# The down product of both feed-forward blocks in seven products, one product after the other over all tokens

## The chip, the cores and the metric

The kernel runs on one NeuronCore of a Trainium2 chip. The metric is the device time of one execution in microseconds (us), from the first instruction to the last output in DRAM. The core has five instruction streams that matter here: PE (matrix products into PSUM banks), DVE and POOL (elementwise work), ACT (elementwise work with functions and row sums) and SP, which only issues DMA transfers. Each stream runs its instructions in order and waits at semaphores for the others. [...]

## The reference

One encoder layer is applied to 1280 tokens (256 of a prompt, 1024 of a sample) of width 1024. What matters here is the feed-forward block, which stands at both ends of the layer:

```python
def swiglu(x, w_gu, w_down):
    g, u = jnp.split(x @ w_gu, 2, axis=-1)
    return (jax.nn.silu(g) * u) @ w_down

x = x + 0.5 * rmsnorm(swiglu(rmsnorm(x, ffn1_pre), ffn1_w_gu, ffn1_w_down), ffn1_post)
...   # attention in two head groups, with projections in and out
x = x + 0.5 * rmsnorm(swiglu(rmsnorm(x, ffn2_pre), ffn2_w_gu, ffn2_w_down), ffn2_post)
x = rmsnorm(x, final_norm)
```

`w_gu` is 1024 x 5632 and `w_down` 2816 x 1024. All inputs and outputs are float32.

## The kernel before

**Numbers.** Every large product takes its float32 operands as a rounded part and a rest (`split`: ACT copies the rounded part, DVE subtracts it from the source), and does three matmuls for one: high x high, high x low, low x high.

**Gate and up phase** (class `GateUp`). The tokens are ten tiles of 128, taken in five pairs; chunk 0 holds two pairs and chunk 1 three, so that a matmul has 256 or 384 columns, one token of each pair in either half. The hidden width is 22 blocks f of 128. For each block and chunk the gate and up product of the two halves of the model width and the two tokens of a pair is done in Strassen's form (Winograd's variant), in seven products j = 0..6 of 12 matmuls: a block is 2 x 7 x 12 = 168 matmuls (L289). The sums of the weight halves are made on DVE during the block before (L258 to L267), and each of seven weight operands is split (L63 on ACT, L66 on DVE). Each product is added from its PSUM bank into an SBUF tile by DVE (L298) or copied by ACT. At j = 5 and 6 the hidden values `w` (the first token of each pair) and `v` (the second) are ready (L312, L317) and stored to DRAM, two DMAs to a chunk, in planes `hd`. SP also issues the next gate and up weights, `raw`, 2 x 512 KB to a block, at the end of a block.

**Down phase** (class `Down`, `down_phase`). The 22 blocks are in four groups `FGROUPS`. The output width is in two halves. For half 0 and then half 1, token tile by token tile, `part` multiplies the four groups of hidden values (`hl` loaded from `hd`, split into `hh` and `hl`) with the weights `wd`, which stay in SBUF for all ten tiles, into one PSUM bank: 2 halves x 10 tiles x 22 blocks x 3 = 1320 matmuls of 512 columns to a phase (L390). Weights arrive as `rawd`, 256 KB each, through two buffers, 44 to a phase. `first_done` takes the sum of squares of half 0 (ACT) and puts it into DRAM (`y0d`). `second_done` and `finish` are a chain by token tile: squares of half 1 (ACT, L163), the row factor (POOL, L171 and L172), the two halves scaled (DVE, L1150, L1151), added to the residual (L1153, L1154), squares of the sum (ACT), a second row factor (POOL) and the scaling with it (DVE: L1258 in the first phase, L1352 in the second). In the first phase the tile is then transposed on PE and split (L76, L77, L81) as operand `xt` of the attention's projection (`pj`, L519), whose weights `mraw` come by SP (L502); in the second phase it is the output.

**Order.** The code is one stream of calls with generators (`yield`) that interleave; a scheduler of the framework then sets the order in each engine's stream, and inserts the waits. A tile of a pool with n buffers waits until the n-th before it has been released. So the order on DVE and SP around a place is read from the built program, as below.

## Time and profile before

| What | us |
|---|---|
| median of 3 runs (lowest, highest) | 2406.21 (2404.09, 2406.82) |
| the profiled execution | 2410.93 |
| its span, first to last instruction | 2409.2 |
| PE busy | 2321.3 |
| DVE busy | 1336.0 |
| ACT busy | 940.9 |
| POOL busy | 393.0 |
| first down phase, first to last matmul | 599 to 917 |
| second down phase, first to last matmul | 2089 to 2397 |

In the lines below, a group of instructions is named by its line in the kernel before, its engine and operation, and output <- inputs by the program's names; then come its count, its busy time, the mean of one in ns, and the idle time ahead of it with what ended it. A timeline row has the start and length in us. A row of windows has the stretch, its length, PE's busy time with the number of matmuls that started in it, the granted clock, the share of time the DMA engines were busy, and GB/s.

### The profile page before, as it was taken

Reading aid. Unit: us, or ns where it says so; the run is one execution under the profiler, and the core shown is the slowest. Engines: PE = TensorE matmul, PEld = TensorE weight load, DVE = VectorE, ACT = ScalarE, POOL = GpSimd, SP = SyncE. Lnnn points to the kernel's source line nnn. Section 1 sums busy time; section 2 is a strip of 40 time slices with the busy share of each in tenths; the row PEclk is TensorE's granted clock in tenths of the full one; section 3 lists DMA queues with packets and bytes.
Section 4 is the critical chain, followed back from the end, with each engine's and each line's share of the span. In section 5 each row is a group of like instructions: output and inputs, shape, how many; then the busy total and the mean of one; then the engine's idle time right before and its main releaser. Section 6 shows DMA issues by size and latency. Waiting matters only on the chain.

```text
span 2409.2 us, 36473 instructions
## 1 busy us (share of the span) xinstructions
PE 2321.3 (96%) x13658; PEld 2119.2 (88%) x13658; DVE 1336.0 (55%) x2459; ACT 940.9 (39%) x1937; POOL 393.0 (16%) x548
## 2 busy tenths in 40 slices
PE   6999999999999998999999898899999999999997
PEld 5999999999778886888888787799999999978885
DVE  7665545555443552697655764755555555552344
ACT  5322222223442332587655754422222233342232
POOL 6000000000000112585433424500000000000011
PEclk9999999999999999999999999999999999999999
DMA  4254344533654552322432454322222223463544
GB/s 137 68 122 106 90 120 114 118 76 103 194 176 156 166 182 87 84 56 64 127 101 74 162 172 155 132 81 62 80 64 77 65 69 91 138 219 113 188 163 135
DMA packets 308514, 282.40 MB, mean 117 GB/s; under 512 B 64816, under 2 KB 248496, under 8 KB 308336
## 3 DMA queue, kind: packets, MB, share of 16 engines
q1 hardware_dynamic: 308336, 280.06, 39.8%
q8 instruction: 108, 1.77, 0.3%
q14 instruction: 70, 0.57, 0.1%
HBM read 207.51 MB, written 75.24 MB: 117 GB/s over the span
## 4 chain that ended last, share of the span: by engine, by line
PE 46%; DMA 5%; DVE 4%; POOL 2%; ACT 2%; issue 2%; SPq 0%; DVEq 0%; POOLq 0%; ACTq 0%
PE gups L289 21%; PE pj L519 9%; PE dps L390 6%; PE yps L984 3%; DMA hl<-hd 2%; PE s_ps L548 2%; PE pt L558 2%; DMA rawd<-in_ffn_w_down_dram 1%; ACT junk L163 1%; PE ssq L969 1%; PE o_ps L675 1%; DMA out_dram<-xr 1%; DVE stk L66 1%; POOL rs L172 1%; DVE sb L531 0%
## 5 line engine op out<-in xcount | busy, mean ns | idle before, releaser
L289 PE MATMUL gups<-xh,ah 128*128 128x256 f32 (+1 forms) x2464 | 763.2, 310 | 7.6 <-ACT ah L63 3.3
L289 PE MATMUL gups<-xh,al 128*128 128x256 f32 (+1 forms) x2464 | 761.7, 309 | 0.0
L289 PE MATMUL gups<-xl,ah 128*128 128x256 f32 (+1 forms) x2464 | 761.2, 309 | 0.0
L390 PE MATMUL dps<-wd,hh 128*128 128x512 f32 x1760 | 547.0, 392 | 5.8 <-ACT wd L63 2.8
L289 PEld LDWEIGHTS gups<-xh,ah 128*128 128x128 f32 x2464 | 468.6, 190 | 10.8 <-ACT ah L63 4.1
L289 PEld LDWEIGHTS gups<-xh,al 128*128 128x128 f32 x2464 | 468.4, 190 | 0.6 <-DVE al L66 0.2
L289 PEld LDWEIGHTS gups<-xl,ah 128*128 128x128 f32 x2464 | 468.7, 190 | 0.0
L390 PEld LDWEIGHTS dps<-wd,hh 128*128 128x128 f32 x1760 | 329.5, 188 | 80.2 <-ACT hh L63 6.6
L390 PE MATMUL dps<-wd,hl 128*128 128x512 f32 x880 | 344.8, 392 | 2.6 <-DVE hl L66 2.3
L66 DVE TENSOR_TENSOR hl<-hl,hh 128x768 fp32r<-128x768 f32 (+1 forms) x160 | 142.2, 891 | 243.0 <-ACT hh L63 211.6
L171 POOL TENSOR_SCALAR rs<-ssq,ss 128x1 f32<-128x1 f32 x20 | 9.5, 475 | 1422.7 <-ACT junk L163 1422.7
L63 ACT ACTIVATE hh<-hl 128x768 fp32r<-128x768 f32 (+1 forms) x160 | 126.7, 793 | 279.7 <-DMA hl<-hd 252.7
L390 PEld LDWEIGHTS dps<-wd,hl 128*128 128x128 f32 x880 | 165.6, 188 | 43.5 <-DVE hl L66 9.6
L63 ACT ACTIVATE ah<-s 128x512 fp32r<-128x512 f32 x176 | 111.0, 631 | 218.9 <-PE gups L289 140.7
L66 DVE TENSOR_TENSOR al<-s,ah 128x512 fp32r<-128x512 f32 x176 | 121.6, 691 | 95.0 <-ACT ah L63 93.8
L519 PE MATMUL pj<-xh,mh 128*128 128x512 f32 (+1 forms) x432 | 162.1, 375 | 1.8 <-ACT mh L63 1.8
L519 PE MATMUL pj<-xh,ml 128*128 128x512 f32 (+1 forms) x432 | 155.6, 360 | 0.0
L519 PE MATMUL pj<-xl,mh 128*128 128x512 f32 (+1 forms) x432 | 155.2, 359 | 0.0
L542 POOL TENSOR_TENSOR sb<-sb,rc 128x384 f32<-128x384 f32 (+1 forms) x160 | 126.3, 810 | 153.5 <-DVE rc L540 140.6
L316 ACT ACTIVATE u<-u 128x256 f32<-128x256 f32 x88 | 41.4, 471 | 254.8 <-DVE u L298 250.8
L63 ACT ACTIVATE ah<-raw 128x512 fp32r<-128x512 f32 x132 | 83.2, 630 | 134.6 <-PE gups L289 126.9
L298 DVE TENSOR_TENSOR u<-u,gups 128x384 f32<-128x384 f32 (+1 forms) x176 | 85.5, 486 | 71.7 <-PE gups L289 70.0
(154 smaller groups left out, 3152.3 us busy)
## 6 DMA issues: line engine op xcount, KB each, us to landing
raw<-in_ffn_w_gu_dram SPq DMA_DIRECT2D x88, 512.0 KB, 4.0
hl<-hd SPq DMA_DIRECT2D x80, 384.0 KB, 3.7
hl<-hd SPq DMA_DIRECT2D x80, 320.0 KB, 3.3
rawd<-in_ffn_w_down_dram SPq DMA_DIRECT2D x88, 256.0 KB, 3.1
tab<-tt SPq DMA_DIRECT2D x24, 384.0 KB, 3.5
hd<-w SPq DMA_DIRECT2D x44, 192.0 KB, 2.2
hd<-v SPq DMA_DIRECT2D x44, 192.0 KB, 2.1
tt<-zd SPq DMA_DIRECT2D x16, 384.0 KB, 6.0
```

Of the source, the lines that this page charges most:

```text
L63: nc.scalar.activation(hi, src, AF.Copy)
L66: (lo_eng or nc.vector).tensor_tensor(lo, src, hi.bitcast(F32), op=ALU.subtract)
L163: c.nc.scalar.activation(junk[:, :x.shape[1]], x, AF.Square, scale=1 / 32, accum_out=ss)
L289: nc.tensor.matmul(ps, w[:, k, :], x[:, k, :], start=new and k == 0 and m == 0, stop=k == 3 and m == 2, skip_group_check=not new)
L298: nc.vector.tensor_tensor(out, x, ps, op=add)
L316: nc.scalar.activation(X["u"], X["u"], AF.Silu)
L390: nc.tensor.matmul(ps, a[:, i, :], b, start=f == 0 and m == 0, stop=f == NFF - 1 and m == 2)
L519: nc.tensor.matmul(ps[:, :n], w[:, kk, :], xs[th][:, kk, :], start=first, stop=last)
L542: nc.gpsimd.tensor_tensor(s, s, rc[:, i:i + 1].to_broadcast(list(s.shape)), op=ALU.mult)
L548: nc.tensor.matmul(o, q, kk, start=z == 0, stop=z == 1)
L558: nc.tensor.transpose(pt[:, b, :], sbs[i][:, b * 128:(b + 1) * 128], c.ident)
L984: nc.tensor.matmul(ps, a[:, j, i * 128:i * 128 + 128], b, start=j == 0 and m == 0, stop=j == 3 and m == 2)
```

## The change

The down product too is done in seven products. With the hidden width in two halves (blocks 0 to 10 and 11 to 21), the output width in two halves, and the two tokens of a pair as the two rows, it is a product of 2 x 2 blocks, and `DOWN7` lists the operands of the seven products: hidden planes `w0`, `v0`, `w1`, `v1` (token of the pair, half) or sums `s1` to `s4` of them, and weight blocks B11, B21, B22 or sums T1 to T4 of them. All sums are made on POOL during the gate and up phase: `sums` for each block f >= 11 and chunk (the planes of block f - 11 are fetched back from DRAM, four additions, four stores), and `weight_sums` for the down weights in each odd block (three loads, four additions of 512 columns, four stores).

The down phase goes product by product (q), within it pair by pair (p), within it in two pieces (m) of 6 and 5 blocks. One product of a pair is 11 x 3 = 33 matmuls into one bank, and DVE adds it into accumulators in SBUF (`plus`; four tiles to a pair). The first 44 weight loads of a phase become 77. The second token of each pair is complete at q = 4, the first at q = 6, and the chain (`tile_done`, `finish`) runs behind these two. In the first phase the transposes of the q = 4 tiles are issued together at part 60, and those of the very last tile inside `mix_attention`, whose first loop takes its third stretch of eight steps before its second. PSUM in this phase is four banks for the products and four for the transposes.

```diff
-FGROUPS = [range(0, 6), range(6, 12), range(12, 17), range(17, 22)]
+HF = NFF // 2
+PIECES = [range(0, 6), range(6, 11)]
+PLANES = ("w0", "v0", "w1", "v1", "s1", "s2", "s3", "s4")
+DOWN7 = [("w0", "B11"), ("s2", "T2"), ("s3", "T3"), ("v1", "T4"), ("s1", "T1"), ("s4", "B22"), ("w1", "B21")]
 ...
@@ GateUp
+            self.store("v", f, ch, X["v"])
+            if f >= HF:
+                self.sums(f, ch)
 ...
+    def fetch(self, f, ch):
+        n = CN[ch]
+        x = self.G.tile([128, 2, 384], F32, name="back", tag="x", bufs=3)
+        self.back = [x[:, i, :n] for i in range(2)]
+        for i, name in enumerate(("w0", "v0")):
+            self.c.nc.sync.dma_start(self.back[i].rearrange("p (r x) -> p r x", x=128), self.plane(name, f, ch))
+
+    def sums(self, f, ch):
+        n, e, sub, add = CN[ch], self.c.nc.gpsimd.tensor_tensor, ALU.subtract, ALU.add
+        x = self.G.tile([128, 2, 384], F32, name="sums", tag=("ga", "gb")[ch], bufs=1)
+        s3, s4 = [x[:, i, :n] for i in range(2)]
+        w0, v0 = self.back
+        w1, v1 = self.X["w"], self.X["v"]
+        e(s3, w0, v0, op=sub)
+        self.store("s3", f, ch, s3)
+        e(v0, v0, v1, op=add)
+        self.store("s1", f, ch, v0)
+        e(w0, v0, w0, op=sub)
+        self.store("s2", f, ch, w0)
+        e(s4, w1, w0, op=sub)
+        self.store("s4", f, ch, s4)
 ...
@@ Down
+    def weight_sums(self, i):
+        nc, w = self.c.nc, self.w_down
+        e, sub = nc.gpsimd.tensor_tensor, ALU.subtract
+        x = self.G.tile([128, 2, 512], F32, name="bx", tag="x", bufs=3)
+        nc.sync.dma_start(x.rearrange("p s d -> p (s d)"), w[i * 128:(i + 1) * 128])
 ...
+        e(b22, b22, b12, op=sub)
+        nc.sync.dma_start(self.td["T3"][i], b22)
+        e(b12, b12, b11, op=sub)
+        nc.sync.dma_start(self.td["T1"][i], b12)
+        e(b11, b22, b11, op=ALU.add)
+        nc.sync.dma_start(self.td["T2"][i], b11)
+        e(b21, b21, b11, op=sub)
+        nc.sync.dma_start(self.td["T4"][i], b21)
 ...
     def part(self, n):
+            for v, (a, b) in enumerate(((hi, wh), (hi, wl), (lo, wh))):
+                nc.tensor.matmul(ps, a[:, k, :], b, start=i == 0 and v == 0, stop=i == HF - 1 and v == 2)
+        if m == 0:
+            return
+        A = self.acc[p]
+        def plus(out, x):
+            if out not in A:
+                A[out] = self.ap.tile([128, 512], F32, name=f"{out}{p}")
+            if x is None:
+                nc.scalar.activation(A[out], ps, AF.Copy)
+            else:
+                nc.vector.tensor_tensor(A[out], A[x], ps, op=ALU.add)
 ...
+        if q == 0:
+            plus("c11", None)
+        elif q == 1:
+            plus("u", "c11")
+        elif q == 2:
+            plus("v", "u")
+        elif q == 3:
+            plus("c21", "v")
+            sq("c21", 0)
+        elif q == 4:
+            plus("v", "v")
+            sq("v", 1)
+            plus("u", "u")
+        elif q == 5:
+            plus("u", "u")
+            sq("u", 2)
+        else:
+            plus("c11", "c11")
+            sq("c11", 3)
 ...
@@ mix_attention
-        for i in range(0, 24, 8):
+        for i in (0, 16, 8):
+            if i == 8:
+                late()
 ...
@@ encoder
+    def block_hooks(gu, f, extra):
 ...
+        def behind():
+            with tc.issue_after(gu.last_load.ins):
+                d.weight_sums(f // 2)
+        if f % 2:
+            hooks[10] = behind
+        if f == NFF - 1:
+            for n, i in ((0, 0), (1, 1), (2, 2), (3, 3), (7, 4), (8, 5), (9, 6), (11, 7), (12, 8), (13, 9)):
+                old = hooks.get(n)
+                hooks[n] = lambda old=old, i=i: (old and old(), d.load_w(0, i))
 ...
@@ down_phase
+        for n in range(len(d.seq)):
+            q, p, m = d.seq[n]
 ...
+            if n == 60:
+                last()
+            if m == 0 and q in (4, 6):
+                t = PAIRS[p][q == 4]
+                x = G.tile([128, D], F32, name="xr", tag="x", bufs=3)
+                nc.sync.dma_start(x, res(t))
+            d.load_h(n + 1)
+            d.load_h(n + 2)
+            d.part(n)
+            while loads and done < (2.2 * (n + 1) if n < 10 else 22 + 1.1 * (n - 9)):
+                loads.pop(0)()
+                done += 1
 ...
@@ finish1
-        xn = G.tile([128, D], F32, name="xn", tag="x", bufs=3)
-        nc.vector.scalar_tensor_tensor(xn, x, r, gain, op0=ALU.mult, op1=ALU.mult)
+        for y, h in halves:
+            nc.vector.scalar_tensor_tensor(y, x[:, h], r, gain[:, h], op0=ALU.mult, op1=ALU.mult)
 ...
+        elif t == PAIRS[-1][0]:
+            th, off = third(t)
+            x = state["xt"][1][th][:, :, off:off + 128].bitcast(F32)
+            for k, y in enumerate(xn):
+                nc.sync.dma_start(x[:, 4 * k:4 * k + 4], y.rearrange("p (k x) -> p k x", x=128))
+            state["xn"][t] = [x[:, 4 * k:4 * k + 4] for k in range(2)]
+            state["late"] = transposes(t)
```

The first place is DVE in the second down phase, at the token tiles near its end. Names: `dps` is a product's bank, `xr` the residual, `y`, `c` and `u` result halves, `rs` a row factor. Before, one tile:

```order
L1150 SCALAR_TENSOR_TENSOR y_22820<-y_22820,rs,ga 128x512 [waits DMAHW0_49,Pool_49]
L1151 SCALAR_TENSOR_TENSOR y_22927<-dps,rs,ga 128x512 [waits Activation_49]
L1153 TENSOR_TENSOR xr<-xr,y_22820 128x512 [waits DMAHW3_49,DMAHW5_49,DMAHW2_49,DVE_49]
L1154 TENSOR_TENSOR xr<-xr,y_22927 128x512 [waits DVE_49]
L66 TENSOR_TENSOR hl<-hl,hh 128x640 [waits DMAHW7_49,PE_49,Activation_49]
L1352 SCALAR_TENSOR_TENSOR xr<-xr,rs,gb 128x512 [waits Activation_49,Pool_49]
L1352 SCALAR_TENSOR_TENSOR xr<-xr,rs,gb 128x512 [waits DVE_49]
```

Now, one pair at q = 6:

```order
L477 TENSOR_TENSOR c_22334<-c_22334,dps 128x512 [waits PE_49]
L71 TENSOR_TENSOR hl<-hl,hh 128x640 [waits DMAHW5_49,Activation_49]
L1263 SCALAR_TENSOR_TENSOR c_22334<-c_22334,rs,ga 128x512 [waits Activation_49,Pool_49]
L1263 SCALAR_TENSOR_TENSOR u_22661<-u_22661,rs,ga 128x512
L1266 TENSOR_TENSOR xr<-xr,c_22334 128x512 [waits DVE_49]
L1266 TENSOR_TENSOR xr<-xr,u_22661 128x512 [waits DVE_49]
L71 TENSOR_TENSOR hl<-hl,hh 128x768 [waits DMAHW0_49,Activation_49]
L1467 SCALAR_TENSOR_TENSOR xr<-xr,rs,gb 128x512 [waits Activation_49,Pool_49]
L1467 SCALAR_TENSOR_TENSOR xr<-xr,rs,gb 128x512 [waits DVE_49]
L477 TENSOR_TENSOR c_22400<-c_22400,dps 128x512 [waits PE_49]
```

The addition of the next pair's product stands behind the last scaling of this pair's chain, with two waits for POOL between; half as many matmuls lie between two tiles as before.

The second place is SP at the end of the first down phase. Before:

```order
L1254 DMA x1d_75<-xr 128x1024 [waits DMAHW0_49,DVE_49]
L575 DMA cos<-in_cosT_dram 128x1024 [waits PE_49]
L577 DMA sin<-in_sinT_dram 128x1024 [waits DMAHW2_49,PE_49]
L579 DMA mA<-in_maskA_dram 128x384 [waits DMAHW3_49]
L1254 DMA x1d_76<-xr 128x1024 [waits DMAHW4_49,DVE_49]
L581 DMA sk<-in_sink_a_dram 128x8 [waits DMAHW5_49]
L502 DMA mraw<-in_w_in_dram 128x8x128 [waits DMAHW6_49,PE_49]
L502 DMA mraw<-in_w_in_dram 128x8x128 [waits DMAHW7_49]
```

Now:

```order
L1369 DMA x1d_69<-xr 128x1024 [waits DVE_49]
L1369 DMA x1d_71<-xr 128x1024 [waits DMAHW5_49,DMAHW4_49,DVE_49]
L1369 DMA x1d_73<-xr 128x1024 [waits DMAHW1_49,DVE_49]
L1382 DMA xl_8581<-c_7053 128x4x128 [waits DMAHW6_49,DVE_49]
L1382 DMA xl_8581<-u_7351 128x4x128 [waits DVE_49]
L678 DMA cos<-in_cosT_dram 128x1024 [waits DMAHW0_49]
L680 DMA sin<-in_sinT_dram 128x1024
L682 DMA mA<-in_maskA_dram 128x384 [waits DMAHW2_49]
L684 DMA sk<-in_sink_a_dram 128x8 [waits DMAHW3_49]
L605 DMA mraw<-in_w_in_dram 128x8x128 [waits DMAHW4_49]
L605 DMA mraw<-in_w_in_dram 128x8x128 [waits DMAHW5_49]
```

The loads of `cos`, `sin`, `mA` and `mraw` stand behind two transfers of the last tile (`xl`), which wait for DVE's last scaling; before, only `sk` and `mraw` stood behind the last tile's `x1d`.

The third place is SP in a block of the second gate and up phase. Before:

```order
L322 DMA hd_135<-w 128x3x128 [waits DVE_49]
L322 DMA hd_136<-v 128x3x128 [waits DVE_49]
L322 DMA hd_133<-w 128x2x128 [waits DMAHW6_49,DVE_49]
L322 DMA hd_134<-v 128x2x128 [waits DMAHW7_49,DVE_49]
L238 DMA raw<-in_ffn_w_gu_dram 128x8x128 [waits DMAHW0_49,DMAHW2_49,DVE_49,Activation_49]
L238 DMA raw<-in_ffn_w_gu_dram 128x8x128 [waits DMAHW3_49,DMAHW1_49,DVE_49]
```

Now, a block with f >= 11:

```order
L336 DMA hd1s_153<-sums 128x2x128 [waits DMAHW2_49,Pool_49]
L243 DMA raw<-in_ffn_w_gu_dram 128x8x128 [waits DMAHW3_49,DVE_49,Activation_49]
L243 DMA raw<-in_ffn_w_gu_dram 128x8x128 [waits DMAHW4_49,DVE_49]
L403 DMA bt<-in_ffn_w_down_dram 128x512
L404 DMA bt<-in_ffn_w_down_dram 128x512
L336 DMA hd1w_138<-w 128x3x128 [waits DMAHW7_49,DVE_49]
L336 DMA hd1v_142<-v 128x3x128 [waits DMAHW0_49,DVE_49]
L336 DMA hd1s_146<-back 128x3x128 [waits DMAHW1_49,Pool_49]
L336 DMA hd1s_150<-back 128x3x128 [waits DMAHW2_49,Pool_49]
L336 DMA hd1s_158<-sums 128x3x128 [waits DMAHW3_49,Pool_49]
L399 DMA bx<-in_ffn_w_down_dram 128x1024 [waits DMAHW4_49,DMAHW2_49,DMAHW1_49]
L336 DMA hd1s_154<-sums 128x3x128 [waits DMAHW5_49,Pool_49]
```

SP carries the sums' stores (`hd1s`), which wait for POOL, and the next loads of `raw` stand behind one of them.

More of the change, by code (lines that the diff above doesn't have):

```diff
@@ L334, in run @@
                 next(nxt, None)
-            if n == 6 and late:
-                late()
+            if n in hooks:
+                hooks[n]()
         for _ in nxt:
@@ L368, in load_h, with tile @@
+        def tile(name):
+            if n == 0:
+                return self.G.tile([128, 6, 128], F32R, name=name, tag="x", bufs=3)[:, :k]
+            return self.hp.tile([128, 6, 128], F32R, name=name, bufs=3)[:, :k]
+        lo, hi = tile("hl"), tile("hh")
+        nc.sync.dma_start(lo.bitcast(F32), self.hd[DOWN7[q][0]][m][ch][p - CHUNKS[ch][0]])
         split(c, hi, lo, lo.bitcast(F32))
         self.sub[n] = hi, lo
-    def order(self, entries):
-        for half, ts in entries:
-            for g in range(4):
-                self.seq += [(half, t, g) for t in ts]
-        self.n, self.ps = 0, {}
@@ L378, in part @@
-    def part(self, n, fs=None):
+    def part(self, n):
         c, nc = self.c, self.c.nc
-        half, t, g = self.seq[n]
+        q, p, m = self.seq[n]
         self.load_h(n)
         hi, lo = self.sub.pop(n)
-        if g == 0:
-            self.ps[t] = c.ps.tile([128, 512], F32, name="dps", tag="y")
-        ps = self.ps[t]
-        for i, f in enumerate(FGROUPS[g]):
-            wh, wl = self.w[half, f][:, 0], self.w[half, f][:, 1]
-            for m, (a, b) in enumerate(((hi, wh), (hi, wl), (lo, wh))):
-                nc.tensor.matmul(ps, a[:, i, :], b, start=f == 0 and m == 0, stop=f == NFF - 1 and m == 2)
@@ L1166, in encoder @@
     c.ps.use(**dict(GATE, tr=(4, 5, 6, 7)))
-    def wd_first(d):
-        for f in range(5):
-            d.load_w(0, f, G, ("x", "x", "x", "ga", "gb")[f], 3 if f < 3 else 1)
     gain = []
@@ L1234, in encoder, with open_xt @@
     for f in range(1, NFF):
-        if f == NFF - 1:
-            with tc.issue_after(gu.last_load.ins):
-                wd_first(gu.down)
-        gu.run(f, behind if late and f > 1 else None)
+        gu.run(f, block_hooks(gu, f, {6: behind} if late and f > 1 else {}))
     L.close(2)
-    R.close(2)
-    d = gu.down
-    d.hp = L.open("h", 1)
-    p0 = L.open("wd0", 1)
-    p1 = R.open("wd1", 1)
-    state = {}
-    def swap():
+    R.close()
+    state = dict(xn={}, late=None)
+    def open_xt():
         L.close(2)
@@ L1250, in swap, with transposes, finish1 @@
         state["xt"] = new_xt(c)
-        d.hp = R.open("h2", 1)
-    def finish1(t, x, gain):
+        for t in state["xn"]:
+            for _ in transposes(t):
+                pass
+    def transposes(t):
+        th, off = third(t)
+        for k, y in enumerate(state["xn"][t]):
+            pt = c.ps.tile([128, 4, 128], F32, name="tr", tag="tr")
+            for j in range(4):
+                src = y[:, j * 128:(j + 1) * 128] if len(y.shape) == 2 else y[:, j]
+                nc.tensor.transpose(pt[:, j, :], src, c.ident)
+            hi, lo = [x[th][:, 4 * k:4 * k + 4, off:off + 128] for x in state["xt"]]
+            nc.scalar.activation(hi, pt, AF.Copy)
+            nc.vector.tensor_tensor(lo, pt, hi.bitcast(F32), op=ALU.subtract)
+            yield 1
+    def finish1(t, x, gain, halves):
         nc.sync.dma_start(x1d[t], x)
```

214 lines of the change are left out of this document (107 added, 107 removed).

## The prediction

> **What bounds the kernel now.** I read the busy table, then windows by stage, then the groups of the down product.
>
> ```profile
> PE 2321.3 (96%) x13658; PEld 2119.2 (88%) x13658; DVE 1336.0 (55%) x2459; ACT 940.9 (39%) x1937; POOL 393.0 (16%) x548
> ```
> ```profile
> 100.00:500.00 400.00, 400.00 (x2723) 398.98 (x2722) 223.24 (x404) 108.25 (x211) 9.14 (x9) 1.00 0.46 108
> 1600.00:2000.00 400.00, 400.00 (x2737) 400.00 (x2737) 223.27 (x405) 110.54 (x209) 0.00 (x0) 1.00 0.24 69
> ```
> ```profile
> L390 PE MATMUL dps<-wd,hh 128*128 128x512 f32 x1760 | 547.0, 392 | 5.8 <-ACT wd L63 2.8
> L390 PE MATMUL dps<-wd,hl 128*128 128x512 f32 x880 | 344.8, 392 | 2.6 <-DVE hl L66 2.3
> ```
>
> PE is busy 96% of the span. The second fence holds windows of all engines (PE, PE's weight loads, DVE, ACT, POOL, then granted clock, DMA share and GB/s) in the two gate and up phases: PE never pauses, POOL is nearly free, DVE is busy 223 of 400 us. The third counts 1760 + 880 = 2640 down matmuls, 1320 to a phase. Their 392 ns overlap, so the price of one comes from windows of the down phases, filtered to these matmuls:
>
> ```profile
> 590.00:610.00 20.00, 10.83 (x46) 1.00 0.39 112
> 610.00:630.00 20.00, 16.82 (x63) 0.91 0.53 157
> 630.00:650.00 20.00, 19.05 (x79) 1.00 0.62 212
> 670.00:690.00 20.00, 19.29 (x84) 1.00 0.63 200
> 690.00:710.00 20.00, 19.86 (x87) 1.00 0.56 187
> 2090.00:2110.00 20.00, 20.00 (x90) 1.00 0.59 188
> 2130.00:2150.00 20.00, 19.68 (x84) 1.00 0.69 223
> 2150.00:2170.00 20.00, 18.52 (x77) 1.00 0.68 223
> 2330.00:2350.00 20.00, 19.65 (x83) 1.00 0.53 178
> 2350.00:2370.00 20.00, 19.56 (x84) 1.00 0.57 188
> 2370.00:2390.00 20.00, 19.26 (x80) 1.00 0.41 137
> ```
>
> An undisturbed window starts 90 in 20 us: 0.2222 us each. Windows with fewer are where PE waits: at a phase's start, for weights and hidden values, and near its end, for the chain by tile.
>
> **The change, part by part.** The sum is made on the profiled execution, 2410.9 us, which lies 4.7 us (0.2%) above the median.
>
> *Removed.* A phase now has 7 products x 5 pairs x 11 blocks x 3 = 1155 matmuls of the same shape, 165 fewer: 165 x 0.2222 = 36.7 us, **-73.3 us** for both phases. PE sets the end there, so all of it would count if nothing else came to the front. The added work of the down phase itself has room: a part of 16.5 matmuls on average is 3.67 us, and DVE's whole phase, priced by the rows below (77 weight splits at 0.69, 70 value splits at 0.89, 40 additions at 0.68, ten chains at 4.3, 20 rests of transposes at 0.69), is about 200 of 257 us.
>
> *Sums on POOL beside DVE in gate and up.*
>
> ```profile
> L66 DVE TENSOR_TENSOR al<-s,ah 128x512 fp32r<-128x512 f32 x176 | 121.6, 691 | 95.0 <-ACT ah L63 93.8
> L66 DVE TENSOR_TENSOR hl<-hl,hh 128x768 fp32r<-128x768 f32 (+1 forms) x160 | 142.2, 891 | 243.0 <-ACT hh L63 211.6
> L258 DVE TENSOR_TENSOR s<-raw 128x512 f32<-128x512 f32 x44 | 33.1, 751 | 7.1 <-DMA raw<-in_ffn_w_gu_dram 6.8
> L312 DVE TENSOR_TENSOR w<-w,g 128x384 f32<-128x384 f32 x44 | 24.3, 553 | 0.2
> ```
> ```profile
> 1474.71 2.41 POOL L1011 TENSOR_TENSOR x<-x,y 128x1024 f32<-128x1024 f32 x1
> 1477.08 2.28 POOL L213 TENSOR_TENSOR t<-x 128x512 f32<-128x512 f32 x1
> 1479.44 1.29 POOL L214 TENSOR_TENSOR t<-x,t 128x512 f32<-128x512 f32 x1
> ```
> ```profile
> 1474.79 3.41 DVE L157 SCALAR_TENSOR_TENSOR x<-x,rs,gb 128x1024 f32<-128x1024 f32 x1 [0.76 <-POOL rs L172]
> 1483.62 1.29 DVE L157 SCALAR_TENSOR_TENSOR x<-x,rs,gb 128x1024 f32<-128x1024 f32 x1 [5.35 <-POOL rs L172]
> ```
>
> A block of 168 matmuls lasts 168 x 400 / 2737 = 24.55 us, with 13.7 us of DVE. POOL's additions cost 1.29 us per 512 columns, so a block with f >= 11 brings 4 x (0.65 + 0.97) = 6.5 us, an odd block 4 x 1.29 = 5.2 us for the weights, odd ones with f >= 11 both, 11.7 us; a phase has 11 x 11.7 = 129 us. The timeline rows show that the two engines hold each other up: DVE's scaling of 1.29 us took 3.41 when POOL's addition had started 0.08 us before it, and POOL's next took 2.28 instead of 1.29. They alternate. About 9.7 us of DVE's block are of this kind (seven `al`, four sums of `raw`, two products to a chunk). If each POOL addition pushes DVE back by its whole length, DVE needs 13.7 + 11.7 = 25.4 us on the six odd blocks with f >= 11: 0.85 over, 5 us to a phase; elsewhere at most 20.2. What remains is latency: an addition from PSUM behind a held instruction, and the `raw` loads behind stores that wait for POOL on SP. Bounds: 0, as half of DVE's time is free, and 22 blocks x (3.41 - 1.29) = 47 us, one hold of full length to each block with f >= 11. I take 5 us to a phase, **+10**, the throughput figure, since each chunk has four banks to wait in. DMA traffic rises from 69 GB/s, 1.7 MB a block, by 1.9 MB for the sums of values and 2.1 MB for those of weights, to 5.7 MB or 232 GB/s in the worst block; the windows of 223 GB/s above had a share of 0.69, so that fits, at nothing.
>
> *Start of the down phases.*
>
> ```profile
> 2100.16 1.35 SPq L351 DMA_DIRECT2D rawd<-in_ffn_w_down_dram  x2
> 2101.56 0.42 SPq L367 DMA_DIRECT2D hl<-hd  x1
> 2104.20 1.94 SPq L351 DMA_DIRECT2D rawd<-in_ffn_w_down_dram  x2
> ```
>
> Before, the windows of the first phase up to 710 lack 4 (from its first matmul at 599 on), 27, 11, 6 and 3 matmuls, 11 us; the second phase lacks (6 + 13) x 0.2222 = 4.2 us. Now SP issues the last block's sum stores, which wait for POOL, ahead of the second part's values: about 5.5 us of POOL's last sums plus a landing, some 7 us against which one part of 4 us is there. Two weights and one value part came every 4.04 us; the first ten parts want 2.2 weights each, 4.4 us against 3.67: 0.8 us lost to a part if the buffers bind all the time, 8 to a phase. With 7 + 3 us to a phase this is 20 against 15, **+4**; bounds -15 (all hidden) and +15 (7 + 8 twice).
>
> *Chain by tile at q = 6.*
>
> ```profile
> 2397.62 0.60 ACT L163 ACTIVATE junk<-dps 128x512 bf16<-128x512 f32 x1 [5.43 <-PE dps L390]
> ```
> ```profile
> 2399.39 0.75 DVE L1150 SCALAR_TENSOR_TENSOR y<-y,rs,ga 128x512 f32<-128x512 f32 x1 [4.80 <-POOL rs L172]
> 2400.72 0.68 DVE L1153 TENSOR_TENSOR xr<-xr,y 128x512 f32<-128x512 f32 x1
> 2404.25 1.41 DVE L1352 SCALAR_TENSOR_TENSOR xr<-xr,rs,gb 128x512 f32<-128x512 f32 x2 [2.25 <-POOL rs L172]
> ```
>
> The last product ends at about 2397.1, and the last scaling 8.5 us later, at 2405.66, through two waits for row factors. With the added 0.7 us of the accumulator, the chain of a pair is 9.3 us. On DVE the next pair's addition stands behind that scaling, so pairs come every 9.3 us, while PE gives one every 33 x 0.2222 = 7.33: 2 us lost to each of four, 8 us, and 0.7 at the kernel's very end. Before, a tile had 66 matmuls, 14.7 us, and still lost (7 + 6 + 10) x 0.2222 = 5 us in the three windows quoted from 2330 on. Second phase: +4. In the first, two rests of transposes come into each pair's chain, partly inside its waits, and before, I see no such loss beyond the transposes: +8. Together **+12**; bounds -5 (the accumulators free PE from the chain) and +22.
>
> *Start of the attention.*
>
> ```profile
> 916.73 0.39 PE L390 MATMUL dps<-wd,hl 128*128 128x512 f32 x1
> 925.36 1.94 PE L76 MATMUL tr<-ident,xn 128*128 128x128 f32 x8 [8.24 <-DVE xn L1258]
> 929.14 0.79 PE L519 MATMUL pj<-xh,mh 128*128 128x512 f32 x1 [1.84 <-ACT mh L63]
> ```
> ```profile
> 922.54 12.61 SPq L502 DMA_DIRECT2D mraw<-in_w_in_dram  x4
> ```
> ```profile
> 928.67 1.33 ACT L63 ACTIVATE mh<-mraw 128x256 fp32r<-128x256 f32 x4 [0.74 <-DMA mraw<-in_w_in_dram]
> ```
>
> Projection began 12.0 us after the last down matmul: `mraw` was issued at +5.4, needed 6.1, and its split opened PE. Now `mraw` stands behind `xl`, which waits for the chain's end at +9.3, and behind `cos`, `sin` and `mA`, five or six issues at some 0.5 us: issued at about +12.5, ready at +18.6, or some 6 us more if the 1.2 MB ahead of it move at 200 GB/s first. Transposes of the last tiles fit in this wait. I take **+8**; bounds +2 and +13.
>
> Sum: 2410.9 - 73.3 + 10 + 4 + 12 + 8 = 2371.6, less 4.7 to stand with the median: **2367 us**.
>
> **The rivals.** *All is covered* (0.17). The slack that DVE and POOL have in the windows speaks for it; the fixed order of DVE at q = 6 and of SP at `mraw` speak against. It gives 2410.9 - 73.3 - 4.7 = 2333, and up to 2345 with small stalls.
>
> *POOL's additions hold DVE so that PE runs dry in gate and up* (0.13). Place: blocks 11 to 21 of both phases. Two engines that alternate, as at 1474.79, make DVE late for the banks; PE, full there today, would show it at once. POOL adds 2 x 129 = 258 us. Without my +10 the sum is 49.3 below today's, so this decides once 19% of POOL's time comes out on PE; at a third, 86 us, the time is 2361.6 + 86 - 4.7 = 2443, slower. [...]
>
> *The down phase runs at the pace of its weights* (0.05). 77 loads go through two buffers. At 4.04 us for two, 156 us of 257, they bind only in the first ten parts. If transfers left over from the sums doubled it there, 10 x 1.1 x 8.1 - 36.7 = 52 us to a phase; at half of that the time is 2367 + 52 = 2419. A milder form is in my range.
>
> *The matmuls don't get fewer, or each dearer*: the program has 33 to a pair and product, of the same shape; no chance of its own.
>
> **How the numbers follow.** My forecast has 0.65, with its own range 2345 to 2392 from the bounds of its four terms taken in part. With the rivals, 2335 to 2405 leaves out 0.05 below and about 0.15 above. A measurement of this kernel can tell some 0.2%, 5 us, from no change. Faster: 0.65 + 0.17 and a little of the second rival, 0.83; slower 0.12; within 0.2% 0.05.
>
> **What would show it.** Down matmuls 2310 in all at 90 to 20 us in mid-phase. Gate and up from block 11 on: PE windows a few us short of full, DVE instructions with two SBUF inputs lengthened beside POOL. At q = 6: additions into `c` about 9.3 us apart. First projection 18 to 22 us after the last down matmul. I am wrong if gate and up windows lose over 2 us to a block, or if the additions at q = 6 come every 7.3 us.

## The result, and the profile after

The changed kernel takes 2501.85 us (median of 4 runs, 2494.44 to 2506.56) against 2405.52 us (2404.09 to 2406.82): a ratio of 1.0398, with a 95% interval of 1.0368 to 1.0428. It is 4% slower; the forecast was 2367 us, between 2335 and 2405. Its profiled execution took 2498.36 us, with a span of 2496.6 us.

The page of the changed kernel, first the busy times, then the groups of the two large products and of one subtraction on DVE (line numbers here and below are those of the changed kernel, but for rows said to be of the kernel before):

```profile
PE 2285.5 (92%) x13328; PEld 2079.7 (83%) x13328; DVE 1441.7 (58%) x2565; ACT 971.5 (39%) x1993; POOL 688.4 (28%) x812
...
L294 PE MATMUL gups<-xh,ah 128*128 128x256 f32 (+1 forms) x2464 | 778.6, 316 | 97.6 <-DVE v L303 53.9
...
L466 PE MATMUL dps<-wd,hh 128*128 128x512 f32 x1540 | 484.0, 395 | 16.4 <-ACT hh L68 16.3
...
L71 DVE TENSOR_TENSOR al<-s,ah 128x512 fp32r<-128x512 f32 x176 | 136.8, 778 | 89.2 <-ACT ah L68 88.4
```

The same gate and up group on the page before:

```profile
L289 PE MATMUL gups<-xh,ah 128*128 128x256 f32 (+1 forms) x2464 | 763.2, 310 | 7.6 <-ACT ah L63 3.3
```

PE has 330 matmuls less, worth 73 us, but is busy only 36 us less, and it waits 97.6 us ahead of the gate and up product, where it waited 7.6 us before. Windows of all engines (PE, weight loads, DVE, ACT, POOL, clock, DMA share, GB/s) show where, first one of the kernel before, then four of the changed kernel:

```profile
400.00:450.00 50.00, 50.00 (x342) 49.81 (x341) 27.00 (x52) 13.18 (x27) 0.00 (x0) 1.00 0.49 118
```
```profile
400.00:450.00 50.00, 35.13 (x210) 33.58 (x208) 17.10 (x28) 7.36 (x15) 8.91 (x9) 0.90 0.49 142
450.00:500.00 50.00, 32.70 (x179) 31.61 (x180) 16.43 (x28) 6.96 (x14) 15.66 (x16) 0.77 0.54 151
...
1750.00:1800.00 50.00, 50.00 (x342) 50.00 (x342) 28.18 (x52) 14.46 (x27) 5.18 (x4) 1.00 0.36 116
...
2050.00:2100.00 50.00, 45.50 (x294) 44.98 (x293) 29.89 (x44) 13.05 (x25) 19.67 (x18) 0.97 0.56 166
```

A full window starts 342 matmuls. In the first gate and up phase 210 and 179 are left, in the second 294, and only in the second half of each phase. No engine is full there. In the two slow windows of the first phase DVE does some 60% of what it did before, and the DMA share is about a half, as it already was before the change. From the first and last matmuls of each stage:

| Stage | before, us | after, us | difference | forecast |
|---|---|---|---|---|
| start to first down matmul | 599.0 | 698.4 | +99.4 | +5 |
| first down phase | 317.7 | 289.2 | -28.5 | -30 |
| its end to the first projection | 12.4 | 27.0 | +14.6 | +8 |
| attention, second gate and up phase | 1159.9 | 1185.8 | +25.9 | +5 |
| second down phase | 308.1 | 279.7 | -28.4 | -28 |
| tail | 12.1 | 16.5 | +4.4 | +1 |

(The forecast's terms for the starts and chains of the down phases, +4 and +12, are put beside the removed matmuls.) The gate and up phases lose 125 us where the forecast had 10. By block, taken from one end of a block to the next (the start of DVE's last product `v<-v,u 128x384`), a block was 24.6 us before. After, blocks 1 to 11 of the first phase are 21 to 29, and then:

```
block          12    13    14    15    16    17    18    19    20    21   sum of 1 to 21 (before)
first phase  32.1  42.4  39.3  42.5  41.0  32.0  32.8  29.5  28.7  28.8   622.6 (521.5)
second phase 23.9  31.3  24.4  30.8  26.6  30.5  23.7  32.2  25.1  28.0   546.0 (517.4)
```

Two patterns, then. In the second phase the odd blocks from 13 on, which make value sums and weight sums, lose 3 to 8 us; the even ones, with value sums alone, 2 at most. In the first phase blocks 12 to 18 lose 7 to 18 us: there the transfers from DRAM to DRAM that write the bias tables of the attention (`tt`, `ttp`) still run, two fills to a block. A fill copies a piece of a prepared table (`zd`) and writes a constant (`in_neg_dram`) beside it.

**An odd block of the second phase.** Timeline rows of the changed kernel around the end of block 15, of SP, then ACT, then PE (`hd1s` takes value sums, `td1T` weight sums, `back` is what is fetched for the value sums):

```profile
2028.14 0.36 SPq L336 DMA_DIRECT2D hd1s<-sums  x1
2028.54 0.47 SPq L410 DMA_DIRECT2D td1T<-bx  x1
...
2031.77 0.43 SPq L243 DMA_DIRECT2D raw<-in_ffn_w_gu_dram  x1
2033.52 0.36 SPq L336 DMA_DIRECT2D hd1s<-sums  x1
2033.93 0.47 SPq L243 DMA_DIRECT2D raw<-in_ffn_w_gu_dram  x1
```
```profile
2037.30 0.63 ACT L68 ACTIVATE ah<-raw 128x512 fp32r<-128x512 f32 x1 [7.22 <-DMA raw<-in_ffn_w_gu_dram]
2037.83 0.51 ACT L321 ACTIVATE u<-u 128x384 f32<-128x384 f32 x1
2038.25 0.36 ACT L306 ACTIVATE u<-gups 128x256 f32<-128x256 f32 x1
```
```profile
2038.66 0.58 PE L294 MATMUL gups<-xh,ah 128*128 128x256 f32 x1 [4.14 <-ACT u L306]
```

DVE's last reads of the two old `raw` buffers ended at 2026.7 and 2029.7, but SP reached the next loads 5 and 4 us later, behind stores of sums that waited for POOL and one fetch after another. ACT's queue then stood 7.2 us at the split of `raw`, with the bank's copy (L306) behind it, for which PE waited. Before, the loads went out within 1 us of the last read, and landed just in time, a median of 3.9 us after they were issued (1900 to 2000 us).

**The first phase.** What ended the waits between 340 and 560 us, and how long transfers took to land between 395 and 440 us (size, then median us):

```profile
POOL sums L353 <- DMA back<-hd0v: 166.4, 10, 34.8
ACT ah L68 <- DMA raw<-in_ffn_w_gu_dram: 90.1, 5, 26.1
...
PE gups L294 <- DVE v L303: 37.1, 5, 10.4
DVE v L303 <- DMA hd0v<-v: 37.0, 3, 15.4
...
DVE v L303 <- POOL back L355: 25.1, 2, 12.6
```
```profile
back<-hd0w SPq DMA_DIRECT2D x2, 192.0 KB, 17.2
...
tt<-in_neg_dram SPq DMA_DIRECT2D x1, 144.0 KB, 19.1
```

POOL waits for the fetched planes, DVE for a free buffer of `v`, which a store or POOL's sum still reads, and PE for DVE. A fetch of 192 KB landed after 17.2 us, while the queue's packets filled 0.46 of the DMA engines' time. In the second phase of the same kernel (`back<-hd1w`, 1900 to 2000 us) it took 2.9, at 0.59.

### The profile page after: what moved, and what is told of

It is laid out like the page before. It is cut to its first block, busy times and chain, and to the rows that moved or that the text cites. A ratio compares the mean times of both kernels' runs of the same rounds, so it can differ in the third digit from the quotient of the medians.

```text
span 2496.6 us, 37097 instructions
## 1 busy us (share of the span) xinstructions
PE 2285.5 (92%) x13328; PEld 2079.7 (83%) x13328; DVE 1441.7 (58%) x2565; ACT 971.5 (39%) x1993; POOL 688.4 (28%) x812
## 5 line engine op out<-in xcount | busy, mean ns | idle before, releaser
L294 PE MATMUL gups<-xh,ah 128*128 128x256 f32 (+1 forms) x2464 | 778.6, 316 | 97.6 <-DVE v L303 53.9
L466 PE MATMUL dps<-wd,hh 128*128 128x512 f32 x1540 | 484.0, 395 | 16.4 <-ACT hh L68 16.3
L466 PEld LDWEIGHTS dps<-wd,hh 128*128 128x128 f32 x1540 | 290.8, 190 | 82.0 <-ACT hh L68 21.3
L466 PE MATMUL dps<-wd,hl 128*128 128x512 f32 x770 | 306.2, 398 | 6.7 <-DVE hl L71 6.3
L71 DVE TENSOR_TENSOR al<-s,ah 128x512 fp32r<-128x512 f32 x176 | 136.8, 778 | 89.2 <-ACT ah L68 88.4
L466 PEld LDWEIGHTS dps<-wd,hl 128*128 128x128 f32 x770 | 146.2, 190 | 47.8 <-DVE hl L71 16.8
L71 DVE TENSOR_TENSOR hl<-hl,hh 128x640 fp32r<-128x640 f32 (+1 forms) x140 | 124.4, 889 | 88.5 <-ACT hh L68 88.2
L71 DVE TENSOR_TENSOR wd<-rawd,wd 128x512 fp32r<-128x512 f32 x154 | 107.3, 699 | 106.3 <-ACT wd L68 105.3
L68 ACT ACTIVATE hh<-hl 128x640 fp32r<-128x640 f32 (+1 forms) x140 | 110.8, 792 | 147.2 <-DMA hl<-hd0s 37.9
L68 ACT ACTIVATE wd<-rawd 128x512 fp32r<-128x512 f32 x154 | 97.0, 631 | 134.5 <-DMA rawd<-in_ffn_w_down_dram 58.1
```

The lines of the kernel that those rows point to most:

```text
L68: nc.scalar.activation(hi, src, AF.Copy)
L71: (lo_eng or nc.vector).tensor_tensor(lo, src, hi.bitcast(F32), op=ALU.subtract)
L294: nc.tensor.matmul(ps, w[:, k, :], x[:, k, :], start=new and k == 0 and m == 0, stop=k == 3 and m == 2, skip_group_check=not new)
L466: nc.tensor.matmul(ps, a[:, k, :], b, start=i == 0 and v == 0, stop=i == HF - 1 and v == 2)
```

## The experiments

The theory from these rows (**queue**): transfers and the order of SP's queue set the loss, through late `raw`, late fetches and held buffers. The rival is the one of the prediction (**lock**): POOL's additions hold DVE. The phase lengths below are again blocks 1 to 21.

| Run | time, us | first phase | second phase |
|---|---|---|---|
| before / the change | 2405.5 / 2501.9 | 521.5 / 622.6 | 517.4 / 546.0 |
| e4_down_alone | 2360.2 | 516.4 | 516.3 |
| e3_no_stores | 2403.9 | 543.9 | 521.3 |
| e7_no_adds | 2435.2 | 576.1 | 518.1 |
| e1_raw_act | 2466.9 | 556.4 | 545.4 |
| e5_weights_early | 2455.8 | 611.8 | 519.3 |
| e6_bias_act | 2482.2 | 594.3 | 542.8 |
| e9_act_pinned | 2482.0 | 629.6 | 518.2 |
| e10_prefetch | 2418.4 | 570.6 | 521.7 |
| e11_both | 2448.7 | 601.4 | 519.4 |
| e2_bias_early | 2504.4 | 632.5 | 545.0 |
| e12_packed | 2454.6 | 608.5 | 520.6 |
| e13_no_fills | 2397.0 | 548.9 | 523.1 |
| e14_neg_plain | 2408.8 | 563.7 | 521.9 |
| e15_weights_two | 2416.2 | 569.8 | 521.4 |
| e16_second_only | 2383.6 | 520.2 | 521.3 |

e3, e4, e6, e7 and e13 were timed once, which is enough for differences of 10 us and more. The phase lengths come from one profiled execution each; where two runs share what a phase does, they agree within 2 us (e5 611.8 and 519.3; e8, below, 610.0 and 520.4).

### Without the sums

```diff
-            if f >= HF:
-                self.sums(f, ch)
-        if f % 2:
-            hooks[10] = behind
```

> No sums, no fetches, no weight sums: the down product runs its seven products on hidden planes and weight blocks as they are, so the result is not the layer's. Every theory that puts the loss into the gate and up phases expects blocks of 24.6 us in both, as before the change, and the gain of the down phases alone: 28 us each, with the start of the attention some 14 us later and the tail 4 us longer, about 2365. If the loss came from elsewhere (the clock, the new order of banks), the time would stay above 2406.

2360.2 us, blocks of 24.6 us in both phases. The whole loss belongs to the sums, 142 us, and the down phases with all that follows them are worth -45. Against the forecast without its +10 (2357) that is 3 us off.

### Additions without stores, and stores without additions

```diff
-        self.store("s3", f, ch, s3)          # e3: all eight stores of sums out
-        e(s3, w0, v0, op=sub)                # e7: all eight additions out
```

> POOL does every addition, with its loads, but no sum is stored; the down product reads the hidden planes and weight blocks in place of the sums, so the result is not the layer's. Queue theory: SP has no store that waits for POOL ahead of raw, so the second gate and up phase loses under 10 of its 29 us; in the first phase, where fetches still queue behind the bias tables' transfers and POOL still holds v, half of the 101 us or more stays. Lock theory: both phases lose as much as in the changed kernel, since POOL and DVE do the same work.

> Every fetch and store of the sums stays, but POOL adds nothing: the loaded tiles are stored as they came, and the down product reads hidden planes and weight blocks in place of sums, so the result is not the layer's. Queue theory: stores wait for a landing instead of for POOL, which is sooner; the second phase loses 0 to 12 of its 29 us; the first keeps a good part (40 or more of 101), because the fetches behind the bias tables' transfers and the stores behind the fetches stay. Lock theory: both phases lose nothing. Theory that the added traffic itself is too much: both lose as much as before.

With every addition on POOL and no store, the second phase is 5 us over the run without sums, the first 28 us: this bounds the lock from above, at some 5 us, where no store meets it. It is there: `al<-s,ah` takes 757 ns on average in e3 and 691 in e4 and e7. But 25 of the second phase's 29 us need the stores too. With every store and no addition the second phase loses 2 us, the first 60: so in the second phase it is stores that wait for POOL, in the first, for more than half, the transfers by themselves. The lock falls as the main cause. The queue theory has the second phase right in both runs; of the first it had half the loss staying without stores, where only 28 us did.

### raw by ACT

```diff
-                self.last_load = self.c.nc.sync.dma_start(r, ...)
+                self.last_load = self.c.nc.scalar.dma_start(r, ...)
```

> Only the issue of the gate and up weights (raw) moves from SP to ACT; sums, their transfers and their order stay. Queue theory (raw stands on SP behind stores that wait for POOL; ACT then waits for raw with the bank evacuations behind it): the odd blocks from 13 on of the second gate and up phase, 28 to 32 us in the changed kernel, fall to 24.6 to 27, so that phase gets 20 to 30 us shorter; in the first phase raw no longer queues behind the bias tables' small transfers either, and of the 101 us lost there at least a third comes back. Total 2420 to 2450. Lock theory (POOL's additions hold DVE): the blocks stay as long as they are, total 2490 to 2510.

The first phase gained 66 us (28 of which the start of the kernel gave back, since block 0 ended 28 us later), the second as good as none: its odd blocks from 13 to 19 stayed at 30 to 32 us, the even ones from 14 on fell to 22 or 23, and block 1 took 33. The total fits neither theory, and the fall of the odd blocks that the queue theory forecast did not come. There ACT itself now stood:

```profile
1999.01 0.47 ACT L310 ACTIVATE g<-gups 128x384 f32<-128x384 f32 x1
2004.41 0.43 ACTq L243 DMA_DIRECT2D raw<-in_ffn_w_gu_dram  x1
2004.89 0.63 ACT L68 ACTIVATE ah<-s 128x512 fp32r<-128x512 f32 x1 [5.41 <-PE gups L294]
```

`raw` went out at 2004.41, though another engine issued it: 0.1 us after SP's store of value sums `hd1s<-sums`, issued at 2002.46, had landed (2004.31). In the built program the two use the same completion counter (`DMAHW4_49`), for which ACT waited until 2004.34. In the rows at 1950.82, 2056.91 and 2110.86 it is the same, 0.1 us each time. So in this run the first load of `raw` still stood behind a store of sums, through the counter and not through SP's queue, and the run does not test what happens without that. The next one tested it otherwise.

### Weight sums away from value sums

```diff
-                d.weight_sums(f // 2)
-        if f % 2:
+                d.weight_sums(f - 1)
+        if f <= HF:
             hooks[10] = behind
```

> The weight sums are made one to a block in blocks 1 to 11 instead of one in each odd block; nothing else changes. If the loss comes where weight sums and value sums meet on POOL and on SP's queue, the odd blocks from 13 on of the second phase (about 31 us) fall to 25 or less, and the 29 us lost there shrink to under 8; in the first phase the same 20 us or so come back, while the meeting with the bias tables (blocks 12 to 18) still costs 50 or more. Total 2445 to 2470. If the value sums alone are what costs, the even blocks would not have been at 24.6, and the total stays at 2490 or more.

Blocks 12 to 20 of the second phase came to 23.4 to 25.3 us and the phase to 519.3: its loss is the meeting of the two kinds of sums, shown by moving one. That it reaches PE through the late `raw` is read from the rows of block 15 and of e1; no run isolates it. The first phase kept 90 us. The same with the last tile transposed directly:

```diff
-        elif t == PAIRS[-1][0]:
...
-            state["late"] = transposes(t)
```

> As the kernel with weight sums in blocks 1 to 11, and besides the last token tile of the first down phase is transposed like the others, without the two transfers that SP waits to issue ahead of the constants and mraw. If these hold the attention's start (27 us after the last down matmul in the changed kernel, 12 before), it comes 5 to 10 us sooner: total 5 to 10 us under the run with early weight sums alone. If the chain of the last pairs sets it, no difference.

The gap before the projection fell from 26.9 to 22.9 us, but the total did not move (2455.75).

### The bias tables' transfers in the first phase

Four runs moved them. To earlier blocks, two steps to a block:

```diff
-        gu.run(f, block_hooks(gu, f, {6: behind} if late and f > 1 else {}))
+        gu.run(f, block_hooks(gu, f, {3: behind, 6: behind} if late and f > 1 else {}))
```

> The bias tables of the first phase are written two steps to a block in blocks 2 to 10 instead of one in blocks 2 to 18, so they no longer run beside the value sums. Queue theory: blocks 12 to 18 of the first phase (32 to 42 us in the changed kernel) come down to the 24.6 to 31 us of the second phase, about 60 us back in all, less what blocks 2 to 10 lose (0 to 25 us); total 2440 to 2465. Lock theory: blocks 12 to 18 keep their length, since POOL's additions are the same; total about 2500.

To ACT's queue, untied:

```diff
-        nc.sync.dma_start(tf[:, :, a, rh, e0 * 32:e0 * 32 + 256], zf...)     # and the others to tt and ttp
+        nc.scalar.dma_start(tf[:, :, a, rh, e0 * 32:e0 * 32 + 256], zf...)
```

> The 88 or so small-packet transfers that write the bias tables (tt, ttp) are issued by ACT instead of SP. Theory of the small transfers (fetched planes and raw stand behind them in one queue and land in 14 to 17 us instead of 4): blocks 12 to 18 of the first phase come down from 32 to 42 us to about 31 or less on odd blocks and 25 on even ones, 50 us back, unless ACT is held at its own issues as SP was (2 to 4 us each), which would give 20 of that away; total 2435 to 2475. If the transfers load the DMA engines rather than the queue, the blocks stay long whichever engine issues them: total about 2500. The second phase must not move.

The first was a miss: blocks 12 to 20 came to 23 to 33 us, but blocks 3, 4, 7, 8, 9 and 11 went to 33 to 47. In e6 the scheduler moved the transfers, which wait for little, up to blocks 0 to 6, which got slow (block 4 took 44.1 us), while blocks 12 to 18 showed 24.4 to 27.9 but for 15 and 17, at 32 and 33: without these transfers the first phase is like the second. Tied to their blocks, still by ACT, with early weight sums:

```diff
-        with tc.issue_after(gu.last_load.ins):
+        with tc.issue_after(gu.last_load.ins), tc.issue_after(gu.last_act.ins):   # ACT's last function of the block
             late.pop(0)()
```

> As the kernel with weight sums in blocks 1 to 11, and the bias tables' transfers are issued by ACT, one fill at a time, each tied behind an ACT instruction of its own block (two fills to a block from block 9 on), so they run beside the value sums as in the changed kernel but in another queue. Theory of the shared queue: fetches and stores of the value sums land in 3 to 5 us again, blocks 12 to 18 (35 to 44 us with early weight sums alone) fall to 24.6 to 28; first phase about 530 to 560 us instead of 612, total 2375 to 2410. If the small transfers load the DMA engines themselves, the landings stay at 10 us and more and the blocks at 35 and more; if ACT is held at its issues, blocks fall to some 30 with ACT named as what PE waits for.

Blocks 9 to 15 took 33 to 45 us. Landings between 360 and 460 us in this run:

```profile
raw<-in_ffn_w_gu_dram SPq DMA_DIRECT2D x6, 512.0 KB, 11.6
tt<-zd ACTq DMA_DIRECT2D x5, 384.0 KB, 6.4
...
back<-hd0w SPq DMA_DIRECT2D x3, 192.0 KB, 13.1
...
tt<-in_neg_dram ACTq DMA_DIRECT2D x2, 144.0 KB, 11.4
```

With the small transfers in ACT's queue, SP's `raw` and 192 KB fetches still land after 11 to 13 us, and the time is 26 us above e5. So the shared queue is not it; what is left is that the transfers meet in the DMA engines, which is inferred; no run shows it by itself. Then a fetch one chunk earlier, which leaves the load and gives it time, and both together:

```diff
-            if j == 0 and f >= HF:
-                self.fetch(f, ch)
+            nf, nch = (f, 1) if ch == 0 else (f + 1, 0)
+            if j == 0 and HF <= nf < NFF:
+                self.fetch(nf, nch)
```

> As the kernel with weight sums in blocks 1 to 11, and the planes that the value sums need are fetched one chunk earlier. If the late landing of the fetch (14 to 17 us) is what holds POOL, and through it the buffers of v, the part of the wait that ends with POOL (23 of about 50 us of DVE's waits for v in blocks 11 to 17) goes, and blocks 12 to 18 fall by 3 to 8 us each; the part that ends with the landing of the store of v (27 us) stays. Total 2420 to 2445. If the stores alone set it, no difference.

> Early weight sums, bias tables by ACT and fetches one chunk earlier together. If the queue theory holds, nothing is left of the loss in blocks 12 to 18 but ACT's own issues: first phase 525 to 545 us, total 2370 to 2395, below the kernel before (2406). If the fetch is no longer late once the small transfers are in another queue, it adds nothing to the run with ACT alone.

The early fetch took 37 us off, to 2418.4 us (1.0064, 1.0038 to 1.0091), with 49 us still lost in the first phase; ACT on top made it 30 worse. Then the first steps of the tables packed into blocks 1 and 2, so that the fills end with block 10:

```diff
-        gu.run(f, block_hooks(gu, f, {6: behind} if late and f > 1 else {}))
+        gu.run(f, block_hooks(gu, f, {n: behind for n in ((3, 6, 9) if f < 3 else (6,))} if late else {}))
```

> Weight sums in blocks 1 to 11, fetches one chunk earlier, the last tile transposed directly, and the bias tables' steps moved up: three of the first six in each of blocks 1 and 2, then two fills to a block in blocks 3 to 10, so that only the 16 small ttp transfers meet value sums. If it is the meeting of the small transfers with the value sums' fetches and stores that cost the rest (570 us in the first phase of the run with early fetches, 522 before the change), blocks 12 to 17 come down from 30 to 39 us to about 25, with 2 to 3 us lost to each of blocks 1 to 10: first phase 530 to 548, total 2375 to 2395, which is faster than the kernel before (2403 to 2407). If the small transfers cost as much beside the weight sums, blocks 3 to 10 rise to 30 and more and the total stays at 2415 or above.

A miss again: blocks 13 to 21 came to 23.5 to 26.4 us, but blocks 6 to 12, most of them with fills and weight sums, to 29 to 35, and block 2 to 53. The small transfers cost beside the weight sums too.

### What of the transfers it is

```diff
-        for lo, hi in ((0, e0), (e0 + 8, 12)):     # 22 writes of the constant, rows of 128 to 512 bytes
...
+    def plain(a):                                  # 8 writes, rows of 3 KB, blocks 2 to 9
```

> Weight sums in blocks 1 to 11, fetches one chunk earlier, last tile direct; of the bias tables only eight plain writes of the constant are left (1.2 MB each in rows of 3 KB, blocks 2 to 9), all fills from the skewed table are left out, so the bias is wrong and the result is not the layer's. If the small transfers are what the sums collide with in the first phase, blocks 11 to 21 come to 24.6 to 26 and the phase to 525 to 540 us (570 with them, 522 before the change); total 2365 to 2385. If something else in the first phase makes the sums dear, blocks 12 to 17 stay at 30 and more.

> The same with all 16 fills from the skewed table and the ttp transfers kept where they were, but the 30 writes of the constant (rows of 128 to 512 bytes, landing in 10 to 19 us) replaced by eight plain ones in blocks 2 to 9: the whole layer again. If the many small rows of the constant load the DMA engines, fetches and stores in blocks 11 to 17 land in some 5 to 8 us and these blocks fall from 30 to 39 to about 26; total 2375 to 2400, faster than before. If the fills' copies from DRAM to DRAM are what loads them, little changes: 2405 to 2420.

```diff
-                d.weight_sums(f - 1)                 # e15: hooks 3 and 10 of blocks 1 to 6
+                d.weight_sums(i[0])                  # 2 f - 2 and 2 f - 1
```

> As that, with two weight sums to a block in blocks 1 to 6 of both phases, so that no fill meets a weight sum. If POOL's additions and their transfers fit twice into a block, blocks 1 to 6 lose under 2 us each and blocks 8 to 11 of the first phase nothing: 2 to 8 us less than the run with one to a block. If two are too many (POOL 10 us, 4 MB more in a block), blocks 1 to 6 of both phases rise to 27 and more and the total is 20 us or more higher.

The writes of the constant into `tt` are 22 in the trace, not 30 as expected above; they move 3.1 of the 9.2 MB of its fills. Without fills, blocks 12 to 21 take 22.9 to 26.2 us: the meeting is the cause there. With the copies back and only the writes of the constant replaced by plain ones in blocks 2 to 9, blocks 14 to 21 take 23.7 to 26.6 (12 and 13 took 31.0 and 33.4); with early fetches and these writes in place (e10) blocks 12 to 16 took 30 to 39. The direct last tile, which e10 lacks, comes after this stage. Blocks 12 to 21 together took 295 us in e10, 271 in e14 and 245 in e13: half of the loss that is left in e10 there is the doing of the short writes of the constant, and the other half that of the copies (and the few transfers to `ttp`), which move twice the bytes. Landings between 340 and 480 us agree: the 128 KB fetches took a median of 17.3 us in e10, 4.4 in e14 and 2.5 in e13, those of 192 KB 5.8, 6.3 and 2.7. Since the plain writes also lie in other blocks, e14 does not tell what makes the short ones dear. What the plain writes cost instead shows beside the weight sums: blocks 5 to 11 at 27 to 32 in e13. e14 comes to 2408.8 us (1.0035, 1.002 to 1.005), still a little slower than before; two weight sums to a block (e15) made it 7 us longer, since they were too many for the first phase (blocks 4 to 7 at 32 to 36).

### The change in the second block alone

The first feed-forward block keeps its old down product; the second has the change with early weight sums and early fetches:

```diff
     gu = GateUp(c, i["ffn1_w_gu"][0], gup, G, hd[0])           # classes of the kernel before
-    gu = GateUp(c, i["ffn2_w_gu"][0], gup, G, hd[1])
+    gu = GateUp2(c, i["ffn2_w_gu"][0], gup, G, hd2[0])         # classes of the change, with the two edits above
```

> The change in the second feed-forward block alone, where no bias tables are written: the first block keeps the down product of the kernel before, the second has the seven products with weight sums in blocks 1 to 11 and fetches one chunk earlier. Stage by stage from the runs so far: the second down phase 27 us shorter, the gate and up phase before it 2 to 4 us longer, the tail 4 us longer, the first phases as before: 2380 to 2390, faster than the kernel before by 0.5 to 1%. If the changed phase is only cheap because the first one had prepared it, or the loss comes back with another place of the buffers, 2400 or more.

2383.61 us (2380.58 to 2388.26), against 2403.54 of the kernel before, run beside it: ratio 0.9921, 95% interval 0.9906 to 0.9936. The second gate and up phase is 521.3 us, 4 over before, and PE's busy time is:

```profile
PE 2287.7 (96%) x13493; PEld 2090.2 (88%) x13493; DVE 1379.5 (58%) x2507; ACT 958.0 (40%) x1965; POOL 536.3 (23%) x680
```

96% of the span as before the change, with 165 matmuls less. Of the kernels here that make all their sums and tables, it is the fastest, below the kernel before and the change.

## Why the prediction was wrong

**Removed matmuls, starts of the down phases, chain at q = 6: right in sum, in part by luck.** -28.5 and -28.4 us measured, -30 and -28 by the terms. The additions into `c` at q = 6 of the second phase come at about the pace forecast, 8.8 us against 9.3:

```profile
2449.46 0.69 DVE L477 TENSOR_TENSOR c<-c,dps 128x512 f32<-128x512 f32 x1 [2.53 <-PE dps L466]
...
2458.25 0.68 DVE L477 TENSOR_TENSOR c<-c,dps 128x512 f32<-128x512 f32 x1
...
2484.64 0.68 DVE L477 TENSOR_TENSOR c<-c,dps 128x512 f32<-128x512 f32 x1
```

But PE was hardly held by it: with four banks it ran ahead, its last matmul began at 2480.1, and the lag of 4 us shows in the tail. By the starts of the matmuls, against 0.2222 us each, the second phase lost 2 us at q = 6, where the sum had 8; the products q = 1 to 5 together lost 12, where the sum had kept about 6 from the kernel before. These two errors offset each other. The first phase lost 6.6 us at q = 6, near the 8 of the sum.

**Start of the attention: right in kind, too small.** +14.6 against +8, and above its bound of +13:

```profile
1005.74 1.09 PE L1362 MATMUL tr<-ident,xl 128*128 128x128 f32 x4 [10.41 <-DMA xl<-c]
...
1014.62 0.80 PE L622 MATMUL pj<-xh,mh 128*128 128x512 f32 x1 [6.54 <-ACT mh L68]
```

The chain ended later than I had it (the transfers of `xl` were issued 15 us after the last matmul, not 9), and then came `cos` to `mraw` as forecast, and behind the split of `mraw` the first projection at 27.0. Without the `xl` transfers (e8) it came at 22.9.

**Sums on POOL beside DVE: the failed step.** I put +10 with bounds 0 and 47; it measured 125, and the prediction's own sign of being wrong, over 2 us lost to a block, came. The lock, which I had sized by throughput at 5 us to a phase, is no more than some 5 us in the second phase of e3, so that size was right. Two kinds of DVE instruction on two SBUF tiles did lengthen from the kernel before to the change (`al<-s,ah` from 691 to 778 ns on average, `s<-raw,s` from 690 to 927), while the additions from PSUM did not (`u<-u,gups`, 128x384: 553 and 552). What I named in half a sentence ("the `raw` loads behind stores that wait for POOL on SP") and gave no price is where I place the 25 us of the second phase that need the stores. For the first, I set the added traffic at nothing because an average share of 0.69 had been carried elsewhere. That average says nothing of landings: a 192 KB fetch went from 3 to 17 us at a share of a half, beside the bias tables' transfers. The first phase's own row (a DMA share of 0.46 at 108 GB/s, against 0.24 at 69 in the second) showed that something was there, and the kernel before already had late landings: between 340 and 480 us its `raw` took a median of 9.7 us, against 3.9 in the second phase. It had no fetch that POOL and DVE waited for. The bound was wrong in the same way: one hold of an instruction to a block, where the wait goes around a ring of SP, DRAM, POOL, a buffer and DVE.

**The rivals.** The second (slower, 2443 at a third of POOL's time, chance 0.13, an estimate of mine) had the place and the sign, by the wrong mechanism. The first, all covered (2333 to 2345), is what e4 shows once its later start of the attention and its longer tail, 19 us together, are taken off: 2341.

## What to carry to other kernels

An engine with free time is no cover if it hands its results to an in-order queue that also carries what the busy engine needs (here POOL, busy 28% of the span, and SP's queue: 25 of the 29 us lost in the second phase needed the stores): for each new transfer, look at what it waits for and at which loads stand behind it. Price a transfer by what lands in the very stretch where it will run (here 9.7 us for `raw` in the kernel before), not by a median of the page (4.0) or an average share of the DMA engines. And where a change has a gain and a price in different stages, a run without the price shows at once what there is to win: here 45 us, of which the second block gave 20 with two moves.

## What the runs showed of the hardware

**One wait cost more than its length.** After PE had stood from 407.2 to 414.7 us in the changed kernel, the next matmuls started 0.32 us apart instead of 0.174, for 4.6 us; windows of 4 us (gate and up matmuls, then granted clock):

```profile
404.00:408.00 4.00, 3.22 (x19) 1.00 0.15 47
408.00:412.00 4.00, 0.00 (x0) 1.00 0.86 252
412.00:416.00 4.00, 1.29 (x4) 0.57 0.61 178
416.00:420.00 4.00, 4.00 (x16) 0.58 0.81 224
420.00:424.00 4.00, 3.36 (x23) 1.00 0.80 237
```

That is 2 us more for this wait. All gate and up matmuls together keep PE busy 1124.8 us, against 1094.0 before with the same count. So about a quarter of the 125 us lost there, 31 us, is matmuls that ran slower; that it is the clock behind such waits throughout is inferred from this one, where the granted clock was 0.57 and 0.58 in the two windows that hold the slow matmuls.

**Short writes of a constant landed late, and so did the transfers beside them, from SP's queue and from ACT's.** 144 KB of the constant in short rows took 19.1 us to land and the 192 KB fetch beside it 17.2, at a DMA share of a half; from ACT's queue it was 11.4 and 13.1. They were late before the change too: a median of 14.1 us for 144 KB, and 14.7 for 48 KB. Such a mean share is no steady half: in the windows of 4 us above it runs from 0.15 to 0.86. Why it is so is open: the runs tell these writes from the copies beside them (384 KB each, 6.0 us before), but not the length of a row from the number of rows or from the place in the phase.
